# First layer of a four-layer trunk: VectorE's order by a reckoning of two engines' progress

## The chip, the core and the metric

One core of a Trainium2 chip runs the whole program. The metric is device time in microseconds, from the start to the end of one execution; less is better. The engines are TensorE (PE, with its weight loads PEld), VectorE (DVE), ScalarE (ACT), GpSimd (POOL) and SyncE (SP), which issues most transfers.

## What is computed

Four decoder layers with a different token mixer each, over 256 rows of 1024 columns in float32. The change concerns the first layer, native sparse attention: 16 heads of 64 columns, four heads to a key head, three branches (compressed, selected, sliding window), gated and added.

```python
def block(i):                                   # nsa_mixer, 64 query rows at a time
    dist = t[:, None] - cmp_end[None, :]
    p_c = masked_softmax(jnp.einsum('bhgqd,bhnd->bhgqn', qb, kcmp) - slopes * dist.astype(f32), dist >= 0)
    o_c = jnp.einsum('bhgqn,bhnd->bhgqd', p_c, vcmp)
    ...
    p_s = masked_softmax(jnp.einsum('bhgqd,bhqkd->bhgqk', qb, ksel) - slopes * dist.astype(f32), dist >= 0)
    o_s = jnp.einsum('bhgqk,bhqkd->bhgqd', p_s, vsel)
    ...
    p_w = masked_softmax(jnp.einsum('bhgqd,bhkd->bhgqk', qb, kwin) - slopes * dist.astype(f32), mask)
    o_w = jnp.einsum('bhgqk,bhkd->bhgqd', p_w, vwin)
    return jnp.stack([o_c, o_s, o_w])
...
o = jnp.sum(gates * outs, axis=0).reshape(B, S, H * dh)
return (o.astype(u.dtype) * jax.nn.silu(z)) @ w_out
```

`kcmp` and `vcmp` are 15 compressed keys and values for each key head, made by a small two-layer network (`compress`). With 256 rows the selected branch takes every block and the window covers all rows, so both are plain causal attention over their own keys and values.

## The kernel before

**Precision.** A float32 weight is split into a high part (ScalarE, L127, `whi`) and a low part (VectorE, L70, `wlo = raw - whi`, 128x1024), and a product is three matmuls (L234 to L236, or L299 to L301 where the weight is the moving operand). Weights pass through five `raw` buffers: a transfer starts when the low part of the weight five places earlier has been computed. High and low parts have eleven buffers each. `advance` loads weights and issues the high parts, `low_parts` and the first steps of a projection issue the low parts.

**Projections as filler.** `push_proj` puts a projection of 256 output columns into the queue `fq` as 16 steps of three matmuls. `run` goes through a list of work items and calls `fill` after each, which pops some steps (`pop`). So TensorE's order is written out: an item, a step or more, an item.

**The units.** `nsa_order` lists eight units (`nsa_unit`), two heads each; two units make a group g, which shares a key head. A unit's front is `first` (score matmuls L886 and L887 of query rows 0 to 127 for both heads, then VectorE's masks L333), `second` and `finish` (rows 128 to 255, one head each). A mask instruction adds the causal mask, takes the minimum and leaves its result for ScalarE's exponential (L335). Score tiles (`S`) have two buffers: the matmuls of a third tile wait until the masks have read the first. A unit's back runs during the next unit: `trans` (transposes L340, evacuated by ScalarE at L166) twice, then `pvs` (products with v at L356 and L359, the compressed branch's share at L928). The normalisation of a unit's probabilities (`scale`: L905, and L911 eight times) is issued by VectorE after the next unit's first masks.

**The compressed branch.** `cmp_front(g)` stands ahead of a group's first unit: scores of the compressed keys (L829), a reduction (L833), and two lists of five VectorE instructions each in `CHALF`, the halves of its softmax. `first` takes the first half, `second` of the group's first unit the second (L847 to L851). The result `cs` is transposed by `cmp_back(g)` (L864) after `second` of the group's second unit.

**VectorE's order.** In this stretch VectorE's order is the order in which the program issues (`st["own"]`, a manual schedule); ScalarE's is set by the scheduler of the tile framework. `later(n, f)` puts f off until n more steps have been popped; `overdue`, called after each step, issues what is due. Low parts are issued at fixed places: one in `second`, one in `finish`, and ahead of the steps that need them.

**The end of the layer.** `Gate.go` multiplies the output by the gate (L393), `split` makes high and low parts of it (L401, L402), and `out_proj` multiplies by eight output weights (`in_a_o`), 24 matmuls of 512 columns for each half of the columns.

Of the kernel before, what the change touches and what calls it, by code (L numbers as in the profile page):

```python
# [25 lines left out]
NMM, NSB = 3, 2  # L26
KO = (0, 4, 1, 5, 2, 6, 3, 7)
# [9 lines left out]
def trunk(ctx, tc, I, out):  # L37
# [27 lines left out]
    st = {"load": 0, "split": 0, "next": 0, "held": 0, "parts": 0, "after": [], "most": len(seq), "own": False}  # L65
# [11 lines left out]
    def later(n, f):  # L77

        if st["own"]:
            waiting.append((plan["count"] + n, f))  # L80
        else:
            f()

    def overdue(everything=False):
        due = [w for w in waiting if everything or w[0] <= plan["count"]]
        for w in due:
            waiting.remove(w)
            w[1]()
        if due:
            overdue(everything)  # L90

# [157 lines left out]
    def pop():  # L249
        fq.popleft()()  # L250
        plan["count"] += 1
        overdue()
# [6 lines left out]
    def need(i):  # L259

        while fq and (i not in ready or plan["count"] < ready[i] + 6):
            pop()

    def push_proj(use, q=fq, idx=None):

        t = {}
        idx = idx or take(2)

        def step(c, k):
            if c == 0 and k == 0:  # L270
                t["o"] = ps.tile([128, 2, 256], F32, name="mm", bufs=NMM)
            for i, at in ((idx[c], 0), (idx[c] + 1, 0)):
                if k == at and i in low:
                    low.pop(i)()
            wh, wl = parts[idx[c]]
            mm3(t["o"][:, c, :], wh[:, k, :], wl[:, k, :], uT[0][:, k, :], uT[1][:, k, :], k == 0, k == 7)
            if k == 7:
                free(idx[c])
                if c == 1:
                    use(t["o"])  # L280
                advance()

        for c in range(2):
            for k in range(8):
                q.append(lambda c=c, k=k: step(c, k))
# [76 lines left out]
    class Gate:  # L362
# [19 lines left out]
        def have_o(self, p):  # L382
            self.o.add(p)
            self.go()
# [332 lines left out]
    def keep_q(o, g):  # L717


        for j in range(2):  # L720
# [3 lines left out]
            with tc.high_priority(offset=EARLY):  # L724
                ACT.activation(hi, o[r], AF.Copy, scale=sc)
            later(5, lambda r=r, other=other, hs=hs, hi=hi, sc=sc: DVE.scalar_tensor_tensor(
                t["q"][other, hs, :], o[r], sc, hi.bitcast(F32), op0=OP.mult, op1=OP.subtract))
# [5 lines left out]
    def compress(q, lp):  # L733
# [8 lines left out]
        if q == 3 and lp == 3:  # L742
# [6 lines left out]
            def cubic():  # L749
# [3 lines left out]
                later(3, lambda: DVE.scalar_tensor_tensor(hid, ht, 1.0, hp, op0=OP.add, op1=OP.mult))  # L753
# [18 lines left out]
    def second_layer():  # L772
        kp = ps.tile([128, 512], F32, name="S", bufs=NSB)
        for k in range(2):
# [5 lines left out]
                                 op1=OP.subtract)  # L780
        vp = ps.tile([128, 256], F32, name="o", bufs=1)
# [4 lines left out]
        for g in range(4):  # L786
            DVE.tensor_tensor(vbd[g], vp[0:60, None, g * 64:(g + 1) * 64].to_broadcast([60, 4, 64]),
                              bm[:, :, None].to_broadcast([60, 4, 64]), op=OP.mult)
# [33 lines left out]
    def cmp_front(g):  # L822
# [8 lines left out]
        cs = CS[g] = work.tile([128, 2, 4, 15], F32, name="cs", bufs=2)  # L831
        two = sc[:, 0:256].rearrange("p (a s n) -> p a n s", s=2, n=16)[:, :, 0:15, :]
# [28 lines left out]
    def cmp_back(g):  # L861
        ptc = ps.tile([128, 4, 128], F32, name="pt", bufs=2)
# [5 lines left out]
    def nsa_unit(p):  # L868
# [8 lines left out]
        def scores_of(b, js):  # L877
# [4 lines left out]
            for j in js:  # L882
# [5 lines left out]
                S[j] = s  # L888
            for j in js:
                for br in range(2):  # L890
# [4 lines left out]
        def finish():  # L895
            scores_of(1, (1,))
            low_parts(1)
# [16 lines left out]
        def trans(br):  # L914
            t["PT", br] = [transpose_p(t["P"][j, br], "a") for j in range(2)]
# [7 lines left out]
        def pvs():  # L923
            pv(0)
            pv(1)
            o = t["o"]
# [5 lines left out]
        def first():  # L932
            scores_of(0, (0, 1))
            mixed(*(x.pop(0) for x in (SCALE, CHALF) if x))

        def second():
            scores_of(1, (0,))
            if CHALF:
                mixed(CHALF.pop(0))
            low_parts(1)  # L940
# [19 lines left out]

    gh = run(nsa_order(), ga)
    low_parts(len(seq))
# [332 lines left out]
```

## Time and profile before

| | |
|---|---|
| median of 3 runs | 576.66 us (576.42 to 577.11) |
| profiled execution | 576.96 us |
| its span, first to last instruction | 575.3 us |
| PE, PEld busy | 558.5 us, 495.9 us |
| DVE, ACT, POOL busy | 417.3 us, 337.8 us, 32.0 us |
| mean granted clock of TensorE | 0.995 |

The times in the trace count from the start of the span. The first layer's units run from about 69 to 158. A row of the timeline gives start and duration of an instruction, its line, what it writes and reads, and in brackets the idle time ahead of it and what ended that. The ends of matmuls are modelled, so starts are the better measure on PE.

### The profile page before, as it was taken

To read this page: it belongs to the slowest core of one execution; us is meant where nothing else is said; L and a number is where in the kernel's file an instruction comes from. 1 tells how busy PE (TensorE), PEld (TensorE's weight loads), DVE (VectorE), ACT (ScalarE), POOL (GpSimd) and SP (SyncE) were. 2 spreads that over 40 slices of the span, in tenths; PEclk is the share of its full clock that TensorE was granted. 3 is DMA by queue.
4 is the path that set the end of the run, shared out by engine and by line. 5 is a ranking of instruction groups with operands and counts; after the bars stand their busy time and mean duration, and the time that the engine had idled before them with its cause. 6 is when DMAs were issued, how large, how long until landed. Compare 5 with 4: busy or idle time off the path is not lost.

```text
span 575.3 us, 10451 instructions
## 1 busy us (share of the span) xinstructions
PE 558.5 (97%) x3930; PEld 495.9 (86%) x3930; DVE 417.3 (73%) x924; ACT 337.8 (59%) x727; POOL 32.0 (6%) x88
## 2 busy tenths in 40 slices
PE   8999979999999999999999999999999999999995
PEld 7997878777788899999988889999988899899984
DVE  6883796798857877777875896758548878788632
ACT  7752777778925566567633573757525755576410
POOL 2300000000001000001060000000000000000000
PEclk9999989999999999999999999999999999999999
DMA  8764632332443595443432577433525784332012
GB/s 305 252 246 158 246 111 75 122 99 78 152 157 138 187 331 212 148 148 111 159 115 95 184 284 267 158 135 122 171 73 179 271 282 147 121 104 71 2 38 73
DMA packets 27779, 90.96 MB, mean 158 GB/s; under 512 B 4560, under 2 KB 5200, under 8 KB 27728
## 3 DMA queue, kind: packets, MB, share of 16 engines
q1 hardware_dynamic: 26144, 86.09, 43.8%
q10 hardware_dynamic: 1584, 4.20, 2.3%
q8 instruction: 31, 0.51, 0.4%
q14 instruction: 20, 0.16, 0.1%
HBM read 89.22 MB, written 1.05 MB: 157 GB/s over the span
## 4 chain that ended last, share of the span: by engine, by line
PE 86%; DVE 7%; issue 4%; ACT 2%; POOL 1%; POOLq 0%; DVEq 0%; ACTq 0%
PE mm L234 15%; PE mm L235 14%; PE mm L236 14%; PE mm L300 8%; PE mm L301 8%; PE mm L299 8%; PE S L350 3%; PE pt L340 3%; PE o L356 2%; DVE wlo L70 2%; DVE P L333 1%; PE o L737 1%; PE mm L542 1%; PE pt L216 1%; DVE P L911 1%
## 5 line engine op out<-in xcount | busy, mean ns | idle before, releaser
L234 PE MATMUL mm<-uth,whi 128*128 128x256 f32 x736 | 218.2, 296 | 0.0
L70 DVE TENSOR_TENSOR wlo<-raw,whi 128x1024 fp32r<-128x1024 f32 (+1 forms) x153 | 183.1, 1210 | 41.2 <-ACT whi L127 39.8
L235 PE MATMUL mm<-utl,whi 128*128 128x256 f32 x736 | 208.4, 283 | 0.0
L236 PE MATMUL mm<-uth,wlo 128*128 128x256 f32 x736 | 208.3, 283 | 0.0
L127 ACT ACTIVATE whi<-raw 128x1024 fp32r<-128x1024 f32 (+1 forms) x153 | 156.9, 1042 | 65.2 <-PE mm L235 34.2
L234 PEld LDWEIGHTS mm<-uth,whi 128*128 128x128 f32 x736 | 140.8, 191 | 14.1 <-issue 13.3
L235 PEld LDWEIGHTS mm<-utl,whi 128*128 128x128 f32 x736 | 141.3, 192 | 0.9
L236 PEld LDWEIGHTS mm<-uth,wlo 128*128 128x128 f32 x736 | 141.0, 192 | 0.0
L300 PE MATMUL mm<-whi,kT 128*128 128x512 f32 x128 | 50.0, 391 | 1.3 <-DVE kT L402 1.3
L299 PE MATMUL mm<-whi,qT 128*128 128x512 f32 x128 | 50.4, 394 | 0.0
L301 PE MATMUL mm<-wlo,qT 128*128 128x512 f32 x128 | 49.9, 390 | 0.0
L299 PE MATMUL mm<-whi,uth 128*128 128x512 f32 (+1 forms) x112 | 42.6, 380 | 0.0
L301 PE MATMUL mm<-wlo,uth 128*128 128x512 f32 (+1 forms) x112 | 42.1, 376 | 0.0
L300 PE MATMUL mm<-whi,utl 128*128 128x512 f32 (+1 forms) x112 | 42.0, 375 | 0.0
L333 DVE CUSTOM_DVE_ANT_0 P<-S,mask 128x128 f32<-128x128 f32 (+1 forms) x96 | 29.1, 352 | 7.7 <-PE S L887 5.4
L335 ACT ACTIVATE P<-P,mxa 128x128 f32<-128x128 f32 (+1 forms) x64 | 28.4, 446 | 10.1 <-DVE mxa L333 10.0
L468 ACT ACTIVATE junk<-mm 128x512 bf16<-128x512 f32 x16 | 9.5, 594 | 40.2 <-PE mm L301 40.2
L340 PE MATMUL pt<-ident,P 128*128 128x128 f32 x180 | 28.0, 280 | 1.7 <-ACT PT L166 0.8
L300 PEld LDWEIGHTS mm<-whi,kT 128*128 128x128 f32 x128 | 24.1, 188 | 6.3 <-DVE kT L402 1.7
L166 ACT ACTIVATE PT<-pt 128x384 f32<-128x384 f32 x58 | 25.9, 482 | 4.6 <-PE pt L340 4.5
L301 PEld LDWEIGHTS mm<-wlo,qT 128*128 128x128 f32 x128 | 24.0, 188 | 5.0
L299 PEld LDWEIGHTS mm<-whi,qT 128*128 128x128 f32 x128 | 24.1, 188 | 4.7
(212 smaller groups left out, 734.1 us busy)
## 6 DMA issues: line engine op xcount, KB each, us to landing
raw<-in_a_t_dram SPq DMA_DIRECT2D x24, 512.0 KB, 4.6
raw<-in_b_t_dram SPq DMA_DIRECT2D x24, 512.0 KB, 4.7
raw<-in_d_t_dram SPq DMA_DIRECT2D x24, 512.0 KB, 4.4
raw<-in_c_t_dram SPq DMA_DIRECT2D x20, 512.0 KB, 4.7
raw<-in_w_dram SPq DMA_DIRECT2D x8, 512.0 KB, 4.4
raw<-in_a_o_dram SPq DMA_DIRECT2D x8, 512.0 KB, 3.5
raw<-in_b_v_dram SPq DMA_DIRECT2D x8, 512.0 KB, 5.7
raw<-in_b_o_dram SPq DMA_DIRECT2D x8, 512.0 KB, 3.5
```

What stands on the lines that cost most here:

```text
L70: st["lo"] = DVE.tensor_tensor(lo, t, hi.bitcast(F32), op=OP.subtract).ins
L127: ACT.activation(hi, t, AF.Copy)
L166: ACT.activation(dst, src, AF.Copy)
L234: PE.matmul(o, sh, mh, start=first, stop=False)
L235: PE.matmul(o, sh, ml, start=False, stop=False)
L236: PE.matmul(o, sl, mh, start=False, stop=last)
L299: PE.matmul(o, sh, wh[:, j, c0:c1], start=k == 0, stop=False)
L300: PE.matmul(o, sl, wh[:, j, c0:c1], start=False, stop=False)
L301: PE.matmul(o, sh, wl[:, j, c0:c1], start=False, stop=k == 7)
L333: DVE.tensor_tensor_reduce(out=P[:, c0:c1], in0=S, in1=mask[:, c0:c1], scale=-slope, scalar=BIG, op0=OP.add, op1=OP.min, accum_out=mx)
L335: ACT.activation(P[:, c0:c1], P[:, c0:c1], AF.Exp, bias=mx, scale=-1.0, accum_out=l)
L340: PE.transpose(pt[:, i, :], P[:, i * 128:(i + 1) * 128], ident)
```

## The change

A reckoning of the progress of TensorE (`clock["pe"]`) and VectorE (`clock["dve"]`) is kept while the units are issued: `pe()` and `dve()` add durations written into the code. While `st["units"]` is set, `overdue` calls `chores`, which issues a due item, or a low part if none is due, only if VectorE's reckoned time with it stays within 0.5 us (`AHEAD`) of TensorE's. The fixed low parts in `second` and `finish` are gone. The second half of the compressed branch is put off by four steps (`later(4, ...)`, tag `("c", g)`); what is still waiting when `cmp_back(g)` comes is issued there by `flush`. The same holds for q's low halves (tag g, flushed by `need`) and for the four block products of the compressed values (L787, tag "vbd"). A low part is added behind the second layer's k and behind the hidden layer. `have_o` calls `go` two steps later.

```diff
 NMM, NSB = 3, 2
+AHEAD = 0.5
 KO = (0, 4, 1, 5, 2, 6, 3, 7)
...
         add(n + "_o", *range(8))
-    st = {"load": 0, "split": 0, "next": 0, "held": 0, "parts": 0, "after": [], "most": len(seq), "own": False}
+    st = {"load": 0, "split": 0, "next": 0, "held": 0, "parts": 0, "after": [], "most": len(seq), "own": False, "units": False}
     raw, parts, low = {}, {}, {}
...
-    def later(n, f):
+    def later(n, f, tag=None, us=0.6):
         if st["own"]:
-            waiting.append((plan["count"] + n, f))
+            waiting.append((plan["count"] + n, f, tag, us))
         else:
...
     def overdue(everything=False):
+        if st["units"] and not everything:
+            return chores()
         due = [w for w in waiting if everything or w[0] <= plan["count"]]
...
             overdue(everything)
+    def flush(tag):
+        for w in [w for w in waiting if w[2] == tag]:
+            waiting.remove(w)
+            dve(w[3])
+            w[1]()
+    clock = {"pe": 0.0, "dve": 0.0, "S": deque([0.0] * NSB), "exp": 0.0, "P": {}}
+    def pe(us, after=0.0):
+        clock["pe"] = max(clock["pe"], after) + us
+        return clock["pe"]
+    def dve(us, after=0.0):
+        clock["dve"] = max(clock["dve"], after) + us
+        return clock["dve"]
+    def chores():
+        while True:
+            clock["dve"] = max(clock["dve"], clock["pe"] - 1.0)
+            due = [w for w in waiting if w[0] <= plan["count"]]
+            us = due[0][3] if due else 1.15
+            if clock["dve"] + us > clock["pe"] + AHEAD or not (due or low):
+                return
+            dve(us)
+            if due:
+                waiting.remove(due[0])
+                due[0][1]()
+            else:
+                low_parts(1)
...
         plan["count"] += 1
+        pe(0.36)
         overdue()
...
             pop()
+        flush(i)
...
                 if k == at and i in low:
+                    dve(1.15)
                     low.pop(i)()
...
             self.o.add(p)
-            self.go()
+            later(2, self.go)
...
             later(5, lambda r=r, other=other, hs=hs, hi=hi, sc=sc: DVE.scalar_tensor_tensor(
-                t["q"][other, hs, :], o[r], sc, hi.bitcast(F32), op0=OP.mult, op1=OP.subtract))
+                t["q"][other, hs, :], o[r], sc, hi.bitcast(F32), op0=OP.mult, op1=OP.subtract), g, 0.77)
         ready[g] = plan["count"]
...
                 ACT.activation(ht, ht, AF.Tanh, scale=math.sqrt(2.0 / math.pi))
-                later(3, lambda: DVE.scalar_tensor_tensor(hid, ht, 1.0, hp, op0=OP.add, op1=OP.mult))
+                def rest():
+                    DVE.scalar_tensor_tensor(hid, ht, 1.0, hp, op0=OP.add, op1=OP.mult)
+                    low_parts(1)
+                later(3, rest)
...
                                  op1=OP.subtract)
+        low_parts(1)
         vp = ps.tile([128, 256], F32, name="o", bufs=1)
...
         for g in range(4):
-            DVE.tensor_tensor(vbd[g], vp[0:60, None, g * 64:(g + 1) * 64].to_broadcast([60, 4, 64]),
-                              bm[:, :, None].to_broadcast([60, 4, 64]), op=OP.mult)
+            later(0, lambda g=g: DVE.tensor_tensor(
+                vbd[g], vp[0:60, None, g * 64:(g + 1) * 64].to_broadcast([60, 4, 64]),
+                bm[:, :, None].to_broadcast([60, 4, 64]), op=OP.mult), "vbd", 0.34)
...
         cs = CS[g] = work.tile([128, 2, 4, 15], F32, name="cs", bufs=2)
+        pe(1.0, clock["S"].popleft())
+        clock["S"].append(dve(0.35, clock["pe"] + 0.2))
         two = sc[:, 0:256].rearrange("p (a s n) -> p a n s", s=2, n=16)[:, :, 0:15, :]
...
     def cmp_back(g):
+        flush(("c", g))
         ptc = ps.tile([128, 4, 128], F32, name="pt", bufs=2)
...
                 S[j] = s
+                pe(0.24 * (b + 1) + 0.1, clock["S"].popleft())
             for j in js:
+                clock["S"].append(dve((0.42, 0.69)[b], clock["pe"] + 0.2))
+                clock["exp"] = max(clock["exp"], clock["dve"]) + (0.8, 1.0)[b]
                 for br in range(2):
...
             scores_of(1, (1,))
-            low_parts(1)
             SCALE.append(scale())
...
         def trans(br):
+            pe(0.7, clock["P"].get(p, 0.0))
             t["PT", br] = [transpose_p(t["P"][j, br], "a") for j in range(2)]
...
         def pvs():
+            if p == 0:
+                flush("vbd")
             pv(0)
             pv(1)
+            pe(2.1)
             o = t["o"]
...
         def first():
+            exp = clock["exp"]
             scores_of(0, (0, 1))
+            if SCALE:
+                clock["P"][p - 1] = dve(2.0, exp)
+            if CHALF:
+                dve(1.3)
             mixed(*(x.pop(0) for x in (SCALE, CHALF) if x))
...
             if CHALF:
-                mixed(CHALF.pop(0))
-            low_parts(1)
+                half = CHALF.pop(0)
+                later(4, lambda: mixed(half), ("c", g), 1.1)
...
+    st["units"] = True
+    clock["pe"] = clock["dve"] = 0.0
     gh = run(nsa_order(), ga)
+    st["units"] = False
     low_parts(len(seq))
```

The order of instructions shows what comes of it. TensorE's order is the same in both kernels, instruction by instruction. VectorE's changes, and ScalarE's (by its scheduler) with it. Line numbers after the change are higher: the masks are L372, the low parts L71, the scaling L956 and L962, the second half L895 to L899, the compressed transposes L913, the block products L832, the tanh gate L481 and L432, the gate's low part L441.

VectorE in group 0, from the second masks of unit 0 (`S_1009`) to the first of unit 1 (`S_1073`), before. `cl` and `cs` are the second half, `wlo` are low parts, `qT` q's low halves, `S_1047` the third scores of unit 0:

```order
L333 ISA P_978,mxa_982<-S_1009,mask_306 128x256
...
L847 TENSOR_REDUCE cl_961<-cs_958 128x8
...
L851 TENSOR_TENSOR cs_958<-cs_958,cl_961 128x120
L70 TENSOR_TENSOR wlo_762<-raw_759,whi_761 128x1024
L726 SCALAR_TENSOR_TENSOR qT_841<-mm_869,cq_304,qT_841 64x2x256 x2
L333 ISA P_979,mxa_982<-S_1047,mask_306 128x256
...
L70 TENSOR_TENSOR wlo_767<-raw_764,whi_766 128x1024
L333 ISA P_1067,mxa_1072<-S_1073,mask_315 128x128
```

The same place after (the tiles are now `S_1006`, `S_1038` and `S_1065`; `v_364` are block products):

```order
L372 ISA P_975,mxa_979<-S_1006,mask_306 128x256
...
L832 TENSOR_TENSOR v_364<-o_937,bm_355 60x256
L71 TENSOR_TENSOR wlo_762<-raw_759,whi_761 128x1024
L372 ISA P_976,mxa_979<-S_1038,mask_306 128x256
...
L832 TENSOR_TENSOR v_364<-o_937,bm_355 60x256 x2
L372 ISA P_1059,mxa_1064<-S_1065,mask_315 128x128
```

The second half and q's low halves are gone from between the second and the third masks.

VectorE in the second unit of group 1 (unit 3), before: the last scaling of unit 2, the second masks of unit 3 (`S_1410`), a low part, the third masks (`S_1479`); the second half of this group stands 27 rows earlier, in unit 2:

```order
L911 TENSOR_SCALAR P_1232<-P_1232,la_1233 128x256
L333 ISA P_1374,mxa_1379<-S_1410,mask_315 128x256
...
L333 ISA P_1375,mxa_1379<-S_1410,mask_315 128x256
...
L70 TENSOR_TENSOR wlo_863<-raw_802,whi_862 128x1024
L333 ISA P_1376,mxa_1379<-S_1479,mask_315 128x256
```

After, at the same place:

```order
L962 TENSOR_SCALAR P_1231<-P_1231,la_1232 128x256
L372 ISA P_1366,mxa_1371<-S_1402,mask_315 128x256
...
L895 TENSOR_REDUCE cl_1220<-cs_1217 128x8
...
L899 TENSOR_TENSOR cs_1217<-cs_1217,cl_1220 128x120
L71 TENSOR_TENSOR wlo_800<-raw_784,whi_799 128x1024
L372 ISA P_1368,mxa_1371<-S_1476,mask_315 128x256
```

TensorE there, after (and, but for names and lines, before): the second scores of unit 3, two steps, and the transposes of `cs_1217`, which L899 above writes.

```order
L935 MATMUL S_1402<-kT_470,qT_841 128x512
L936 MATMUL S_1402<-tu_471,qT_841 128x512
L270 MATMUL mm_1287<-uth_88,whi_776 128x256
L271 MATMUL mm_1287<-utl_89,whi_776 128x256
L272 MATMUL mm_1287<-uth_88,wlo_777 128x256
L270 MATMUL mm_1287<-uth_88,whi_776 128x256
L271 MATMUL mm_1287<-utl_89,whi_776 128x256
L272 MATMUL mm_1287<-uth_88,wlo_777 128x256
L913 MATMUL pt_1420<-ident_77,cs_1217 60x128 x2
```

The second half now stands behind the scaling and the second masks, in groups 0, 2 and 3 too (in group 0 with one low part more ahead of it).

VectorE at the end of the units, before: gate (`zw`, L442 and L393) and its low parts (`kT`) for the last quarter, then low parts of weights, the first of them of the seventh output weight (`raw_1187`):

```order
L402 TENSOR_TENSOR kT_2012<-oT_868,qT_2011 128x512 x3
...
L442 SCALAR_TENSOR_TENSOR zw_2111<-zw_2111,mm_1981 128x512
L393 SCALAR_TENSOR_TENSOR oT_868<-oT_868,zw_2111 128x512
L402 TENSOR_TENSOR kT_2012<-oT_868,qT_2011 128x512
L70 TENSOR_TENSOR wlo_1709<-raw_1187,whi_1708 128x1024
```

After (`raw_839` is the first output weight, `raw_1031` the fifth):

```order
L441 TENSOR_TENSOR kT_2006<-oT_869,qT_2005 128x512
L71 TENSOR_TENSOR wlo_1108<-raw_839,whi_1107 128x1024
L71 TENSOR_TENSOR wlo_1180<-raw_865,whi_1179 128x1024
L71 TENSOR_TENSOR wlo_1283<-raw_900,whi_1282 128x1024
L481 SCALAR_TENSOR_TENSOR zw_2108<-zw_2108,mm_1975 128x512
L432 SCALAR_TENSOR_TENSOR oT_869<-oT_869,zw_2108 128x512
L441 TENSOR_TENSOR kT_2006<-oT_869,qT_2005 128x512
L71 TENSOR_TENSOR wlo_1357<-raw_967,whi_1356 128x1024
L71 TENSOR_TENSOR wlo_1449<-raw_1031,whi_1448 128x1024
```

The low parts of the first six output weights have moved from inside the units to behind their last scaling.

## Rows read from the trace of the kernel before

**Rows 1.** The page: busy time and share; clock over the span's 40 slices; exponentials.
```profile
PE 558.5 (97%) x3930; PEld 495.9 (86%) x3930; DVE 417.3 (73%) x924; ACT 337.8 (59%) x727; POOL 32.0 (6%) x88
...
PEclk9999989999999999999999999999999999999999
...
L335 ACT ACTIVATE P<-P,mxa 128x128 f32<-128x128 f32 (+1 forms) x64 | 28.4, 446 | 10.1 <-DVE mxa L333 10.0
```

**Rows 2.** PE's waits, 60 to 165: who for whom, us in total, times, longest.
```profile
PE S L886 <- DVE mxa L333: 4.3, 5, 2.1
PE pt L340 <- ACT PT L166: 0.8, 2, 0.4
```

**Rows 3.** Timeline of PE in group 0: start us, duration us, instruction.
```profile
77.18 0.28 PE L887 MATMUL S<-tu,qT 128*128 128x256 f32 x1
79.56 0.36 PE L886 MATMUL S<-kT,qT 128*128 128x256 f32 x1 [2.11 <-DVE mxa L333]
...
83.00 0.63 PE L864 MATMUL pt<-ident,cs 128*60 128x128 f32 x2
...
86.22 0.82 PE L340 MATMUL pt<-ident,P 128*128 128x128 f32 x6
```

**Rows 4.** Timeline of DVE in group 0.
```profile
69.04 1.41 DVE L787 TENSOR_TENSOR v<-o,bm 60x256 f32<-60x256 f32 x4 [0.63 <-PE o L784]
...
74.69 0.27 DVE L847 TENSOR_REDUCE cl<-cs 128x8 f32<-128x120 f32 x1
...
75.64 0.28 DVE L851 TENSOR_TENSOR cs<-cs,cl 128x120 f32<-128x120 f32 x1
```

**Rows 5.** Stretch 81 to 85: busy us of each engine, granted clock, DMA share, GB/s.
```profile
81.00:85.00 4.00, 3.88 (x18) 3.70 (x19) 3.93 (x19) 3.23 (x11) 0.00 (x0) 0.57 0.38 135
```

**Rows 6.** Timeline of DVE in unit 3.
```profile
104.64 0.28 DVE L333 CUSTOM_DVE_ANT_0 P<-S,mask 128x128 f32<-128x128 f32 x1
...
105.48 0.20 DVE L905 RECIPROCAL la<-la 128x8 f32<-128x8 f32 x1
...
107.77 0.41 DVE L333 CUSTOM_DVE_ANT_0 P<-S,mask 128x256 f32<-128x256 f32 x1
...
108.45 1.22 DVE L70 TENSOR_TENSOR wlo<-raw,whi 128x1024 fp32r<-128x1024 f32 x1
```

**Rows 7.** Timeline of PE in units 3, 5 and 7.
```profile
105.28 0.47 PE L886 MATMUL S<-kT,qT 128*128 128x512 f32 x1 [0.80 <-DVE mxa L333]
...
106.54 0.38 PE L864 MATMUL pt<-ident,cs 128*60 128x128 f32 x2
...
110.60 0.40 PE L886 MATMUL S<-kT,qT 128*128 128x512 f32 x1
...
125.44 0.47 PE L886 MATMUL S<-kT,qT 128*128 128x512 f32 x1 [0.63 <-DVE mxa L333]
...
144.75 0.47 PE L886 MATMUL S<-kT,qT 128*128 128x512 f32 x1
...
145.64 0.38 PE L864 MATMUL pt<-ident,cs 128*60 128x128 f32 x2
...
148.93 0.40 PE L886 MATMUL S<-kT,qT 128*128 128x512 f32 x1
...
153.40 0.82 PE L340 MATMUL pt<-ident,P 128*128 128x128 f32 x6
```

**Rows 8.** Instructions on the raw weights, 55 to 165: ns least, median, most.
```profile
L127 ACT ACTIVATE whi<-raw x25: 1040/1049/1071, 57.0 to 160.8; 128x1024 fp32r<-128x1024 f32 x25
...
DMA to landing us min/median/max: 3.4/3.5/5.3
```

**Rows 9.** Timelines of PE and DVE in the output projection.
```profile
165.30 0.39 PE L301 MATMUL mm<-wlo,qT 128*128 128x512 f32 x1
...
165.18 5.76 DVE L70 TENSOR_TENSOR wlo<-raw,whi 128x1024 fp32r<-128x1024 f32 x5
```

## Prediction

> **Names.** In the first layer eight units of two heads run in four groups, 0 to 3; a group's two units share a key head. A unit's scores come in three parts: F1 (query rows 0 to 127, both heads), F2 and F3 (rows 128 to 255, one head each, 512 columns). T0 and T1 are the two transposes of a unit's probabilities, run during the next unit. Each group has one compressed branch, whose softmax is two halves on VectorE (five instructions each). Its result, `cs`, is transposed by L864 after F2 of the group's second unit. A step is one entry of the projection queue: three matmuls.
>
> **What bounds the kernel now.** I read the page's engine shares first: TensorE is busy for 97% of the span and VectorE for 73% [rows 1]. So only TensorE's waits, and the time its clock is halved, can be won, and a delay counts when TensorE stands behind it. Next come TensorE's waits in the first layer [rows 2]: five before scores, 4.3 us, all ended by VectorE, and two before transposes, 0.8 us. The longest lies in group 0. TensorE has issued the first pair of score matmuls of unit 1 at 77.18 and gets the next score buffer only at 79.56 [rows 3]. On VectorE at that time stand the second half (74.69 to 75.92), a weight's low part and two q low parts [rows 4], and only behind them the F3 masks that free the buffer. After this wait the granted clock falls: its mean over 81 to 85 is 0.57 [rows 5], so about 3.4 of these 4 us ran at the lower level of 1.2 GHz, half of the upper one, and 1.7 us of work was lost.
>
> **Part 1: the second half moves behind the next unit's scaling.** The order of the changed kernel shows it at the same place in all four groups: not in a gap of VectorE, but by the flush ahead of the compressed transposes. It stands behind the second unit's F1 masks, the scaling of eight blocks and the F2 masks. TensorE's order is unchanged, so L864 must wait for that chain. I cost it in group 1, where every link has a row. Let s be the start of the F1 masks of unit 3, 104.64. The reciprocal and the scaling start at 105.48, the F2 masks at 107.77, and the instruction behind them at 108.45, s+3.81 [rows 6]. The half lasts 1.23 us (74.69 to 75.92, [rows 4]), so L864 can start at s+5.04. TensorE starts F2 at 105.28, s+0.64, and L864 1.26 us later, s+1.90 [rows 7]. New wait: 3.14 us. In groups 2 and 3 there is one step instead of two between F2 and L864 (144.75 to 145.64 is 0.89 us, [rows 7]), and the wait is 3.51 us each. Sum for groups 1 to 3: 10.2 us. It can't be hidden by VectorE running ahead, because s itself waits for TensorE's F1.
>
> Some of it is given back. While TensorE stands, ScalarE and VectorE catch up. The 0.63 us wait before F2 in group 2 [rows 7] goes, since no low parts stand ahead of its F1 masks any more; group 1 keeps its 0.80, because the gate product L393 now stands ahead of F1 and waits for the output of unit 1. From L864 to F3 takes 4.06 us in group 1 (106.54 to 110.60) and 3.29 in group 3 (145.64 to 148.93) [rows 7]; with T1's waits on evacuations and scaling gone I take 3.7 and 2.6, and 2.6 in group 2 as well, which returns 0.4 + 0.7 + 0.7. Net for groups 1 to 3: 10.2 - 0.6 - 1.8 = 7.8 us; bounds 6 and 10.2 (nothing returned).
>
> **Part 2: group 0.** Here the change does what its reckoning aims at. Between the F2 and F3 masks of unit 0 stand only one block product (1.41 us for four, [rows 4]) and one low part, so the three waits of this group go, 2.9 us (the 4.3 of [rows 2] less the 0.80 and 0.63 of groups 1 and 2, [rows 7]), and TensorE reaches L864 by 79.3: 83.00 [rows 3] less 2.9 and 0.8 for the part of the cold stretch that lies ahead of it. VectorE's queue to the end of the half, counted from the end of the F2 masks of unit 0 (74.69 before, about 0.8 earlier now, since three of the four block products moved behind): three block products 1.05, two low parts 2.3 (five take 5.76, [rows 9]), F3 masks 0.68 (as F2's, [rows 6]), F1 masks 0.84, reciprocal and scaling 2.29, F2 masks 0.68, the half 1.23, together 9.07. That is 82.9 to 83.8. L864 starts where it started before, 83.0, and the gain ahead of it is spent. Behind it, T1 can't beat 86.4: the second low part now ends at about 81.9 and releases the transfer of a raw weight; that lands 3.5 us later, its high part takes 1.05 us on ScalarE [rows 8], and in ScalarE's new order it stands ahead of the evacuation that T1 needs. T1 was at 86.22 [rows 3], so group 0 costs +0.2 at least, and +1.4 if the clock falls once more. I take +0.7.
>
> **Part 3: low parts left over.** Before, six of the eight output weights have their low part ahead of the units' last scaling; now the first stands behind it. Two things follow. In unit 7 the F3 exponentials stand behind a high part on ScalarE whose transfer is released by the low part after the half of group 3: L864 + 1.15 + 3.5 + 1.05, then two exponentials of 0.45 [rows 1] and half of the 2.29 for reciprocal and scaling make T0 at L864 + 7.8. Before, it was 7.76 (145.64 to 153.40, [rows 7]), and 7.1 with the 0.7 returned in part 1. That is +0.7. In the output projection the fifth output weight is read at 165.30; the run of low parts behind the last gate split starts at 165.18 [rows 9], and its low part is now the second of that run: 165.18 + 2 x 1.15 = 167.5. That is 2.2 us of waiting, or 1.4 if the gate chain, freed of the high part ahead of it on ScalarE, comes 0.8 earlier. I take 1.9. Sum +2.6; bounds 0.5 (both covered by other slack) and 4.
>
> **Part 4: the clock.** The one wait above 2 us was followed by 3.4 us at half clock, and none of the other waits, 0.8 us or less, was [rows 2]: the clock row of the page has its only lower digit there [rows 1]. The three new waits of 3.1 to 3.5 us are longer than the one that cost 1.7. I charge two of three, 3.5 us; bounds 0 and 5.2. The Trainium skill (TensorE: Matmul & The Clock Gate, section "HAM oscillation — how this bites in real kernels") describes a loop in which every wait for data is followed by a cold start and takes half of each throttled stretch as the penalty. By it all four waits of this kernel would be charged, group 0 too, and the sum would be some 2.4 us higher; the one case in this trace agrees with its price, and whether every wait falls cold no row here shows.
>
> **The sum.** 7.8 + 0.7 + 2.6 + 3.5 = 14.6 us on the profiled execution of 576.96, that is 591.6. That execution lies 0.3 above the median of 576.66, so I predict 591.3.
>
> **Rivals.** (a) The clock holds in groups 1 to 3 and the tail is covered: 7.8 + 0.2 + 0.5 = 8.5 us, 585. For it: a wait's fall in clock is seen once only. Against: the new waits are longer than that one.
>
> (b) Faster: L864's wait vanishes, because VectorE stands so far ahead that the half is done when TensorE arrives, and the waits before scores go with the cold stretch: 4.3 + 0.8 + 1.7 = 6.8 us at most, 570. The point from which it decides: the half would have to end by s+1.90, yet the scaling and F2 masks ahead of it alone end at s+3.81. VectorE's idle stretches do exist, but they lie behind L864, and the half isn't put there. 5%.
>
> (c) The change doesn't do what it says and no time moves: the half is put by a flush, not by the reckoning, and each new wait is paid by an old one as in group 0; 577. Groups 1 to 3 have only 1.4 us of such waits before scores, so this holds for group 0 alone. 4%.
>
> **How the numbers follow.** Forecast 66%, (a) 25%, (b) 5%, (c) 4%. The forecast's own range: 6 + 0.2 + 0.5 + 1.7 = 8.4 at the low end, 10.2 + 1.4 + 4 + 5.2 = 20.8 at the high end, hardly all at once. The range reaches down through (a) and stops at 582; up to 598. A measurement of this kernel can tell about 0.2% from no change. Faster 5%, same 4%, slower 91%.
>
> **What would show it.** Right: L864 waits some 3 us for VectorE's L851 in groups 1 to 3 and about 4 in group 0; the 2.1 us wait at 77 is gone; VectorE's idle time before F3 masks grows; the clock shows stretches of 0.5 behind the waits; the first low-part wait in the output projection is on the fifth weight. Wrong: if L864 starts less than 1.5 us behind its step, the chain of part 1 is mis-sized. If the clock stays at 1.00 in groups 1 to 3, part 4 falls and (a) is the time. If the output projection has no wait for a low part, part 3 is halved.

## The result, and the profile after

The changed kernel takes 596.46 us (594.41 to 598.10 in four runs), the kernel before 576.54 beside it: a ratio of 1.0342, with a 95% interval of 1.0326 to 1.0358. The profiled execution took 597.39 us, 20.43 more than that of the kernel before (576.96).

The page of the changed kernel, busy time and granted clock, against [rows 1]:

```profile
PE 565.5 (95%) x3930; PEld 502.1 (84%) x3930; DVE 417.4 (70%) x924; ACT 340.2 (57%) x727; POOL 32.0 (5%) x88
...
PEclk9999979898899899999999999999999999999999
```

VectorE does the same work (417.3 before) and has more idle time; TensorE's share falls. Where the clock row had one low digit, it now has five, all in the first layer and at its end (a slice is 14.9 us).

TensorE's waits from 60 to 200, who for whom, us in total, times, longest, against [rows 2]:

```profile
PE pt L913 <- DVE cs L899: 14.2, 4, 4.2
PE pt L252 <- DVE tu L243: 2.0, 1, 2.0
PE mm L340 <- DVE wlo L71: 1.4, 1, 1.4
PE S L935 <- DVE mxa L372: 1.1, 2, 0.8
```

L913 are the compressed transposes (L864 before), L899 is the last instruction of the half (L851 before). Their four waits are the first row; they did not wait at all before. The 2.1 us wait of [rows 3] before the scores of unit 1 is gone, as are two more of [rows 2].

VectorE in unit 3, start and duration, against [rows 6]:

```profile
106.62 0.28 DVE L372 CUSTOM_DVE_ANT_0 P<-S,mask 128x128 f32<-128x128 f32 x1
...
107.26 0.20 DVE L956 RECIPROCAL la<-la 128x8 f32<-128x8 f32 x1
...
109.54 0.41 DVE L372 CUSTOM_DVE_ANT_0 P<-S,mask 128x256 f32<-128x256 f32 x1
...
110.23 0.27 DVE L895 TENSOR_REDUCE cl<-cs 128x8 f32<-128x120 f32 x1
...
111.18 0.28 DVE L899 TENSOR_TENSOR cs<-cs,cl 128x120 f32<-128x120 f32 x1
111.38 1.22 DVE L71 TENSOR_TENSOR wlo<-raw,whi 128x1024 fp32r<-128x1024 f32 x1
117.51 0.42 DVE L372 CUSTOM_DVE_ANT_0 P<-S,mask 128x256 f32<-128x256 f32 x1 [4.91 <-PE S L936]
```

The chain is the one the prediction reckoned: F1 masks, scaling, F2 masks, the half at 110.23. Its result is there at 111.46; TensorE had reached the transposes at 108.49. The last row shows what that buys: VectorE then stands idle for 4.91 us, waiting for the F3 scores that TensorE could not reach. VectorE's lateness is made by its order, not by its load.

What followed each wait, by the granted clock (1.00 is 2.4 GHz, 0.50 is 1.2 GHz; columns as in [rows 5]):

```profile
112.00:116.00 4.00, 4.00 (x23) 4.00 (x23) 0.60 (x1) 2.01 (x6) 0.00 (x0) 0.58 0.42 131
136.00:140.00 4.00, 4.00 (x23) 3.96 (x23) 0.95 (x1) 2.25 (x5) 0.00 (x0) 0.59 0.38 130
160.00:164.00 4.00, 4.00 (x23) 3.99 (x22) 0.64 (x1) 2.58 (x6) 0.00 (x0) 0.61 0.43 161
```

Each mean stands for more than three of the four us at the lower level, and in group 0 the clock was at 0.50 from 83.2 to 88. And there is a place the prediction doesn't speak of, the border between the first layer and the second. Timelines of ScalarE, VectorE and TensorE there:

```profile
187.28 2.17 ACT L163 ACTIVATE whi<-raw 128x1024 fp32r<-128x1024 f32 x2 [5.12 <-DMA raw<-in_b_v_dram]
189.35 0.58 ACT L507 ACTIVATE junk<-mm 128x512 bf16<-128x512 f32 x1
...
188.38 2.36 DVE L71 TENSOR_TENSOR wlo<-raw,whi 128x1024 fp32r<-128x1024 f32 x2 [3.29 <-ACT whi L163]
190.65 0.15 DVE L509 TENSOR_SCALAR poh<-ss 128x1 f32<-128x1 f32 x1
...
197.18 1.07 PE L252 MATMUL pt<-ident,tu 128*128 128x128 f32 x4 [2.01 <-DVE tu L243]
```

The squares of the output (L507) and the chain of the norm (L509) stand in ScalarE's and VectorE's order behind the high and low parts of the second layer's first weights (`in_b_v`), which wait for their transfers. TensorE waits 2.01 us for the result, and the clock falls once more (0.66 over 198 to 202).

### The profile page after: what moved, and what is told of

Read it like the earlier page. It is cut to its first block, busy times and chain, and to the rows that moved or that the text cites. A ratio compares the mean times of both kernels' runs of the same rounds, so it can differ in the third digit from the quotient of the medians.

```text
span 595.7 us, 10434 instructions
## 1 busy us (share of the span) xinstructions
PE 565.5 (95%) x3930; PEld 502.1 (84%) x3930; DVE 417.4 (70%) x924; ACT 340.2 (57%) x727; POOL 32.0 (5%) x88
## 4 chain that ended last, share of the span: by engine, by line
PE 80%; DVE 9%; issue 4%; DMA 3%; ACT 2%; POOL 1%; POOLq 0%; DVEq 0%; SPq 0%; ACTq 0%
PE mm L270 15%; PE mm L271 13%; PE mm L272 13%; PE mm L339 7%; PE mm L340 7%; PE mm L338 7%; PE pt L379 4%; PE S L389 3%; PE o L395 2%; DVE P L372 2%; DVE P L962 2%; DVE wlo L71 1%; PE o L776 1%; DMA raw<-in_b_v_dram 1%; PE pt L252 1%
## 5 line engine op out<-in xcount | busy, mean ns | idle before, releaser
L71 DVE TENSOR_TENSOR wlo<-raw,whi 128x1024 fp32r<-128x1024 f32 (+1 forms) x153 | 182.7, 1210 | 43.8 <-ACT whi L163 42.8
L372 DVE CUSTOM_DVE_ANT_0 P<-S,mask 128x128 f32<-128x128 f32 (+1 forms) x96 | 29.1, 352 | 25.1 <-PE S L936 22.9
L379 PE MATMUL pt<-ident,P 128*128 128x128 f32 x180 | 31.1, 303 | 0.7
L507 ACT ACTIVATE junk<-mm 128x512 bf16<-128x512 f32 x16 | 9.5, 592 | 31.2 <-PE mm L340 31.2
```

The source lines that it names most:

```text
L71: st["lo"] = DVE.tensor_tensor(lo, t, hi.bitcast(F32), op=OP.subtract).ins
L372: DVE.tensor_tensor_reduce(out=P[:, c0:c1], in0=S, in1=mask[:, c0:c1], scale=-slope, scalar=BIG, op0=OP.add, op1=OP.min, accum_out=mx)
L379: PE.transpose(pt[:, i, :], P[:, i * 128:(i + 1) * 128], ident)
```

## The experiments

**Theory A**: the time is TensorE's wait for the half, which stands behind the second unit's scaling and F2 masks, and the half clock behind each wait. **Theory B**: the later low parts of the weights hold up transfers and high parts, and the waits at L913 only show it. Ratios are to the kernel before on the same chip (medians 577.03, 577.33 and 577.23 us), with 95% intervals.

| Kernel | us | ratio |
|---|---|---|
| e1, half at once | 576.89 | 1.0001 [0.9990, 1.0013] |
| e2, half late, alone | 599.82 | 1.0392 [1.0375, 1.0410] |
| e3, low parts back | 599.25 | 1.0390 [1.0345, 1.0436] |
| e4, both back | 575.28 | 0.9975 [0.9965, 0.9985] |
| e5, wait filled | 592.62 | 1.0263 [1.0247, 1.0278] |
| e6, transposes behind T1 | 582.08 | 1.0087 [1.0070, 1.0104] |
| e7, half at once, 1.0 us ahead | 573.25 | 0.9933 [0.9919, 0.9948] |
| e8, half ahead of the scaling | 574.99 | 0.9963 [0.9950, 0.9975] |
| e9, only 1.0 us ahead | 579.92 | 1.0045 [1.0031, 1.0060] |
| e10, e8 and 1.0 us ahead | 573.78 | 0.9943 [0.9930, 0.9955] |

### One part undone, one part alone (e1, e2)

```diff
 # e1, in second(), against the changed kernel
-                half = CHALF.pop(0)
-                later(4, lambda: mixed(half), ("c", g), 1.1)
+                dve(1.1)
+                mixed(CHALF.pop(0))
 # e2, against the kernel before: in second(), then ahead of and in cmp_back()
-                mixed(CHALF.pop(0))
+                t_half[g] = CHALF.pop(0)
...
+    t_half = {}
+
     def cmp_back(g):
+        mixed(t_half.pop(g))
```

> The changed kernel with one part undone: the second half of a compressed softmax is issued right behind the F2 masks of the group's first unit, as in the kernel before; block products, query low parts and weight low parts stay under the reckoning. Theory A (the half behind the next unit's scaling and F2 masks makes TensorE wait, and the clock falls behind each such wait): the four waits of the compressed transposes, 14.2 us in the changed kernel, go, and with them the stretches at half clock in groups 1 to 3, 13.3 us in all by the shift of the scores of the trace; group 0 even gains up to 3 us, since its waits before scores stay away; the loss behind the layer (output projection 1.6, layer border 4) remains. Time 576 to 581 us. Theory B (the weights' low parts, later in VectorE's queue, hold up the transfers and high parts, and the waits of the compressed transposes only show it): the time stays at 590 us or more.

> The kernel before with one part of the change alone: the second half is issued ahead of the compressed transposes, behind the second unit's scaling and F2 masks. Low parts and everything else keep their fixed places, so a low part of a weight still stands behind the F2 masks and now ahead of the half. Theory A: the compressed transposes wait 3 to 4.5 us in all four groups, a stretch at half clock follows each wait, and the time is 588 to 596 us, with no wait in the output projection and none of 2 us at the layer border. Theory B: 577 to 581 us, because the low parts come in time.

e1 has no wait at L913 and, in the profiled execution, no low digit in its clock row. TensorE's waits from 60 to 200:

```profile
PE S L935 <- DVE mxa L372: 3.0, 3, 2.2
PE pt L252 <- DVE tu L243: 1.1, 1, 1.1
...
PE mm L340 <- DVE wlo L71: 0.2, 1, 0.2
```

One instruction group moved back takes away the whole loss of 20 us. The loss behind the units, which I expected to stay at 5.6 us, shrank to 2.5: from the F3 scores of unit 7 to the transposes at the border (L252) it takes 32.04 us, against 29.53 in the kernel before, with a wait of 0.2 us and one of 1.1 without half clock. So more than half of that loss was a consequence of the late half too. Why is not shown; a late half may take the room in which the reckoning would have handed out low parts, but only one more of them stands ahead of the last gate split (14 against 13). The scores of group 3 come 3 us earlier than before, and most of that is lost again by the border. e2 is the reverse, the half late and nothing else:

```profile
PE pt L867 <- DVE cs L851: 17.5, 4, 4.5
PE S L889 <- DVE mxa L333: 2.1, 4, 1.0
```

It loses 22.8 us, more than the whole change and more than the 588 to 596 expected, with no wait in the output projection and none at the border. The reason for the larger waits is in VectorE's order, here in unit 5:

```profile
138.43 1.22 DVE L70 TENSOR_TENSOR wlo<-raw,whi 128x1024 fp32r<-128x1024 f32 x1
139.57 0.27 DVE L847 TENSOR_REDUCE cl<-cs 128x8 f32<-128x120 f32 x1
```

A low part at its fixed place stands ahead of the half, 1.14 us here (waits of 4.53 and 4.54 in groups 2 and 3 against 3.40 and 3.39; 4.16 in group 1 against 3.12). So theory B falls twice: the half alone makes the loss, and the half alone takes it away.

### The low parts at their places (e3, e4)

```diff
 # chores(): no low parts; both kernels
-            if clock["dve"] + us > clock["pe"] + AHEAD or not (due or low):
+            if clock["dve"] + us > clock["pe"] + AHEAD or not due:
                 return
...
 # finish(), and the same two lines at the end of second()
+            dve(1.15 if low else 0.0)
+            low_parts(1)
 # rest() in compress(), second_layer()
-        low_parts(1)
 # e4: and second() as in e1
```

> The changed kernel with the weights' low parts at the fixed places of the kernel before (one behind the F2 masks and one behind the F3 masks of every unit), the half still late. Theory A: the wait for the fifth output weight and the wait at the layer border with its stretch at half clock go, 5.3 to 5.6 us; the waits of the compressed transposes stay or grow by 1.15 us where a low part now stands ahead of the half. Time 590 to 594 us. Theory B: 580 us or less.

> The changed kernel with both undone: half at once and low parts at their fixed places; block products and query low parts are still put off until they are needed. Theory A: no losses are left, and the gain of the change is seen alone: the 2.9 us of waits before scores in group 0 and the 1.7 us of its cold stretch go at least in part. Time 572 to 576 us, against 576.5 before. Theory B gives no time below that of the kernel before.

e3 missed: 599.25 us, with times from 596.35 to 602.17. What was expected to go did go: its trace (of the execution of 596.35) has no wait for a low part in the output projection and none at the border. But other waits came:

```profile
PE pt L908 <- DVE cs L894: 13.4, 3, 4.5
PE o L392 <- DVE v L827: 2.3, 1, 2.3
PE S L870 <- DVE qT L762: 1.4, 2, 0.9
```

With low parts at fixed places the halves of groups 0, 2 and 3 have one ahead of them, and a block product (L827) and query low parts (L762) come too late; in group 1 the half is issued ahead of the second unit's F1 masks, and nothing waits for it. What separates e3's four times no trace shows; the mean granted clock is 0.977 in the first two and 0.971 and 0.972 in the others (601.10 and 602.17). e4 gives 575.28 us, inside 572 to 576: a quarter of a per cent below the kernel before. That is what the rest of the change is worth without the late half. The gain lies in group 0: from the F2 scores of unit 0 to the F3 scores of unit 1 it takes 12.41 us (74.45 to 86.86), against 15.13 before (72.46 to 87.59), and no clock falls there (the clock row of its page is all nines). The profiled execution, at 576.91 us the longest of ten, had come 2 us late to the units.

### The clock by itself (e5)

```diff
 # cmp_back(), against the changed kernel
         ptc = ps.tile([128, 4, 128], F32, name="pt", bufs=2)
+        for _ in range((36, 26, 28, 28)[g]):
+            PE.transpose(ptc[:, 2, :], ident, ident)
```

> The changed kernel with TensorE kept busy while its compressed transposes wait: ahead of them it runs 36, 26, 28 and 28 transposes of the identity (groups 0 to 3, about 0.1 us each at full clock) into a part of the same PSUM tile that nobody reads. Extra work that is not needed; the half still comes late. It takes the clock alone out of the loss. Theory A with the clock as a price of its own: the stretches behind the four waits run at full clock, which gives back some 1.6 us in each of groups 1 to 3 and 1.5 to 2 in group 0. Time 588 to 592 us. If the granted clock costs nothing, because VectorE and ScalarE set the pace behind the wait: 595 to 598 us.

TensorE in unit 3, and the stretches behind the waits of groups 1 to 3:

```profile
106.23 3.00 PE L913 MATMUL pt<-ident 128*128 128x128 f32 x26
109.53 0.38 PE L915 MATMUL pt<-ident,cs 128*60 128x128 f32 x2 [0.30 <-ACT P L374]
```

```profile
110.00:114.00 4.00, 4.00 (x35) 3.90 (x33) 0.65 (x2) 2.67 (x6) 0.00 (x0) 1.00 0.39 137
132.00:136.00 4.00, 3.77 (x29) 3.30 (x29) 1.56 (x3) 2.93 (x7) 0.00 (x0) 1.00 0.37 119
155.00:159.00 4.00, 4.00 (x34) 3.38 (x35) 0.66 (x1) 3.41 (x8) 0.00 (x0) 1.00 0.37 91
```

The clock stays at 1.00, so the clock's share can be read off group by group. Start of the F3 scores of each group's second unit:

| unit | before | after | e5 | after minus e5 |
|---|---|---|---|---|
| 1 | 87.59 | 89.12 | 87.03 | 2.09 |
| 3 | 110.60 | 116.84 | 113.21 | 3.63 |
| 5 | 129.62 | 140.07 | 135.08 | 4.99 |
| 7 | 148.93 | 163.79 | 157.43 | 6.36 |

The clock takes 2.1, 1.5, 1.4 and 1.4 us in the four groups, 6.4 together. What is left of the shift in e5, 8.50 us by unit 7, is the waits alone. The time of the profiled executions fell by 4.59 us (597.39 to 592.80; the medians, each less that of the kernel before on its own chip, by 4.63), less than 6.4. Most of the rest is given back to later waits. At the border ScalarE's wait for the transfer of `in_b_v` grew from 5.12 to 6.42 us and TensorE's from 2.01 us to this row's, and in the output projection TensorE's grew from 1.40 to 1.58:

```profile
PE pt L252 <- DVE tu L243: 3.1, 1, 3.1
```

### Where the half, or its reader, has to stand (e6, e8)

```diff
 # e6, nsa_order()
             if p % 2:
-                order.append(lambda p=p: cmp_back(p // 2))
-            order += [*b[:2], f[2], b[2]]
+                order.append(lambda p=p: flush(("c", p // 2)))
+            order += b[:2]
+            if p % 2:
+                order.append(lambda p=p: cmp_back(p // 2))
+            order += [f[2], b[2]]
 # e8, first()
             scores_of(0, (0, 1))
+            if p % 2:
+                flush(("c", g))
             if SCALE:
```

> The changed kernel with TensorE's order altered at one place: the half is still put off and flushed ahead of the second unit's T0, as before, but the compressed transposes stand behind T1 instead of ahead of T0, so that T0 and T1, whose blocks are scaled ahead of the half, run while VectorE does the half. Theory A (the wait costs because the compressed transposes stand ahead of work that could run): the waits of the compressed transposes shrink below 1 us, no stretch at half clock is left in groups 1 to 3, and the time is 576 to 583 us. Rival: T0 waits for the scaling as long as the compressed transposes did, since VectorE is what is late; 588 us or more.

> The changed kernel with the half still put off to the group's second unit but flushed behind its F1 masks, ahead of the scaling of the eight blocks: 3 us earlier in VectorE's queue than in the changed kernel, a whole unit later than in the kernel before. By theory A it ends 2.1 us behind the start of the F1 masks, and TensorE reaches the compressed transposes 1.9 us behind it: waits of 0 to 1 us, no half clock, and at most 1.2 us a group because the scaling, and T0 with it, now stands behind the half; 577 to 583 us. If being put off by a unit is what costs, wherever it stands: 588 us or more.

e6 leaves the half as late as it was in groups 0 to 2, by the flush, and gives TensorE T0 and T1 to do meanwhile; in group 3 the reckoning, whose course is altered by this, places the half itself behind the masks of the group's first unit. Its waits, 60 to 200:

```profile
PE S L935 <- DVE mxa L372: 2.8, 2, 2.4
PE mm L340 <- DVE wlo L71: 1.3, 1, 1.3
PE pt L252 <- DVE tu L243: 1.2, 1, 1.2
PE pt L913 <- ACT P L374: 0.9, 1, 0.9
PE pt L913 <- DVE cs L899: 0.7, 1, 0.7
```

No wait at L913 is above 0.9 us and the time is 582.08, inside 576 to 583: most of what the late half cost came from its reader standing ahead of work that could run. Not all of it went: e6 is 0.87% above the kernel before. Its F3 scores of unit 7 start at 148.85 (148.93 before, but 143.61 in e8), and the transposes at the border at 182.10 (178.46), so against the kernel before the loss lies behind the units. In e8 the half of groups 0 and 2 is flushed 3 us further ahead in VectorE's queue, still in the second unit; those of groups 1 and 3 the reckoning now places behind the F3 masks of the first unit. It has 574.99 us, two us below what was expected and 0.4% below the kernel before. Its only wait of this kind:

```profile
PE pt L913 <- DVE cs L899: 0.4, 1, 0.4
```

So in the two groups where the half still stands in the second unit, being put off costs nothing that shows; what cost was that it stood behind the scaling and the F2 masks.

### One number (e7, e9, e10)

```diff
 # e9, against the changed kernel; e10 is e9 with the edit of e8, e7 with that of e1
-AHEAD = 0.5
+AHEAD = 1
```

> The half at once, as in e1, and the reckoning lets VectorE run 1.0 us ahead of TensorE instead of 0.5, which hands out 18 low parts ahead of the last gate split where e1 hands out 14 and the kernel before 16. In e1 the scores of group 3 came 3 us earlier than in the kernel before and the layer border gave 2 of them back to two low parts that stood ahead of the norm's chain. If the late low parts are what takes the gain back: no wait at the layer border, 573 to 575.5 us. If not, or if the low parts ahead delay the masks: 576 us or more.

> The changed kernel with one number altered: the reckoning lets VectorE run 1.0 us ahead of TensorE instead of 0.5. In its order the halves of groups 1 to 3 are then put by the reckoning, between the masks of the group's first unit, and no longer by the flush; only that of group 0 still comes behind the second unit's scaling. Low parts ahead of the last gate split: 18, against 13 in the changed kernel and 16 in the kernel before. Theory A (the loss hangs on where the half lands, and the tail on the low parts left over): one wait of the compressed transposes is left, that of group 0, 4.3 us with its half clock; none in groups 1 to 3; no wait above 1 us at the layer border; 575 to 579 us. If putting the half off costs by itself: 585 us or more.

> As e9 (1.0 us ahead), and a half that the reckoning has not placed by then is flushed behind the F1 masks of the second unit, ahead of the scaling, as in e8; that concerns group 0 alone. Theory A: no compressed transposes wait over 1 us, no half clock in the layer, no wait at the border; 572.5 to 574.5 us, level with e7 (573.25). Otherwise, if a half put off keeps a price: 575 us or more.

In the code, an item of 1.1 us is handed out when VectorE's reckoned time plus 1.1 is at most TensorE's plus `AHEAD`. With 0.5 VectorE must be reckoned 0.6 us behind TensorE when the half is first among the due items, and in the changed kernel that happens in no group before the flush; with 1.0 it takes 0.1. In e9 the half of group 1 goes between the F2 and the F3 masks of unit 2, where VectorE was idle, and those of groups 2 and 3 behind the F3 masks of units 4 and 6. VectorE in unit 2:

```profile
101.05 0.09 DVE L372 DVE_READ_ACCUMULATOR2_ANT mxa<- 128x1 f32 x1
101.80 0.28 DVE L895 TENSOR_REDUCE cl<-cs 128x8 f32<-128x120 f32 x1 [0.66 <-ACT cs L893]
...
103.01 0.42 DVE L372 CUSTOM_DVE_ANT_0 P<-S,mask 128x256 f32<-128x256 f32 x1
```

One wait is left of four, that of group 0, whose half still comes by the flush, with its half clock; and none is left in the output projection or at the border (16 low parts stand ahead of the last gate split, as in the kernel before; I had expected 18):

```profile
PE pt L913 <- DVE cs L899: 4.3, 1, 4.3
PE pt L379 <- ACT PT L202: 0.6, 2, 0.4
```

579.92 us is just above the 575 to 579 expected. e10 takes that last wait too and has 573.78 us: the difference, 6.1 us, is the price of a single late half in group 0 (4.26 us of wait and a clock of 0.56 over the 6 us behind it; the F3 scores of unit 1 start at 90.08 and 84.01), with nothing ahead of it that swallows a part. e7 reaches 573.25 us by the other way, with the half at once. The two longest rows of e10's waits from 60 to 200 and its clock row:

```profile
PE S L935 <- DVE mxa L372: 0.7, 2, 0.6
PE S L819 <- DVE P L808: 0.4, 1, 0.4
...
PEclk9999999999999999999999999999999999999998
```

e7 and e10 beat both kernels, by 0.67% and 0.57% against the kernel before. In e1 (`AHEAD` 0.5) 14 low parts stood ahead of the last gate split and the time was that of before; in e7 18 do, and the wait at the border is gone. From the F3 scores of unit 7 to the border's transposes it takes 32.04 us in e1, 29.74 in e7 and 29.53 before. That the late low parts took back e1's gain is borne out by this pair.

## Why the prediction was right, and where it was not

Predicted 591.3 us, measured 596.46, inside the range of 582 to 598 and slower, by the mechanism named. By its terms, on the profiled executions (20.4 us apart; the medians are 19.9 apart):

| Term | predicted | measured |
|---|---|---|
| Part 1, groups 1 to 3, without the clock | 7.8 | 9.1 |
| Part 2, group 0, without the clock | 0.7 | -0.6 |
| Part 3, T0 of unit 7 | 0.7 | 0 |
| Part 3, fifth output weight | 1.9 | 1.6 |
| Part 4, clock in the groups | 3.5 | 6.4 |
| Layer border | none | 4.0 |
| Sum | 14.6 | 20.4 |

**Part 1** held link by link: waits of 3.12, 3.40 and 3.39 us against 3.14, 3.51 and 3.51. What TensorE gets back behind them is seen in e5, without the clock: L915 to F3 takes 3.68, 2.85 and 2.85 us, against 3.7, 2.6 and 2.6. The net is taken from the table of e5 (8.50 at unit 7, less -0.56 at unit 1) and is 1.3 above the forecast: groups 2 and 3 got back 0.44 us each and not 0.7, the 0.63 us wait before F2 in group 2 was said to go and stayed at 0.35, and some 0.5 us lie in small steps that I did not separate.

**Part 2**: the wait of L913 was 4.25 us ("about 4"), and it started at 83.22 against 83.0. The three waits ahead went, and L913 was where it had been. Behind it the forecast was 0.7, between 0.2 with the clock holding and 1.4 with a fall. Measured are 1.53 with the fall and -0.56 without it (e5): the bound by which T1, behind a raw weight's transfer, could not come earlier was too high (86.4; it starts at 85.66 in e5), and the clock's part too low. Parts 1 and 2 together, 8.5 us both forecast and measured, agree by luck: two errors cancel.

**Part 3**: the wait on the fifth output weight came as forecast, 1.40 us and a shift of 1.57. The 0.7 for T0 of unit 7 did not come: T0 kept its distance to the F3 scores (the shift is 14.86 at both; in e5 8.50 and 8.74), though a high part does stand ahead of the F3 exponentials on ScalarE. The step that failed here is its end: the low parts left over were counted to the last output weight and not beyond. The same lateness reaches the next layer's first weights, whose high and low parts the orders place ahead of the norm's chain at the border. L252 starts 2.3 us later than by the shift before it (197.18 and 178.46 against 16.43), and the half clock behind that wait takes another 1.7: 4.0 us in all (0.66 over the 4 us from 198 makes 1.4 of it). That it hangs on the low parts being late is borne out by e3 and e9, in which they come early enough and the border has no wait, and by e5, where TensorE comes earlier and waits longer.

**Part 4** was mis-sized in number, not in price. The price of 1.7 us read from the one cold stretch of the kernel before stands between the 1.4 and 2.1 measured. I charged two waits; all four were followed by the lower level, and the one at the border too. The loop that the Trainium skill describes, which the prediction set beside its own count (TensorE: Matmul & The Clock Gate, section "HAM oscillation — how this bites in real kernels"), is one in which each wait for data is followed by a cold start. For these four waits it was the better forecast: with the 2.4 us more that the prediction named for it, 3.5 becomes 5.9, and the trace has 6.4. Shorter waits did not follow it every time (see the end). Rival (a), in which the clock holds, falls with part 4.

Rivals (b) and (c) did not come about, for the reason given: in the changed kernel the flush placed every half. With one number changed (e9) the reckoning places the halves of groups 1 to 3, and their waits go, as (b) has it: VectorE's idle stretches, which the prediction saw only behind L864, also lie between and behind the masks of the group's first unit. A time below the kernel before takes group 0 as well (e10).

In all, the forecast of 14.6 us fell short of the 20.4 by the clock (2.9) and the border (4.0), and came inside its range by the range's width, which had been reckoned without the border.

## What to carry to other kernels

An order made by a reckoning is as good as its slack: look in the order at whether an item was placed by the reckoning or by its deadline, and let the deadline stand ahead of the long work that follows, not behind it. When an engine of secondary load is made to finish something late, look for what the bound engine has queued behind the reader; moving the reader behind other ready work took away most of the loss here (e6), moving the writer all of it (e1, e8). Follow lateness past the end of the stage: what is left over there stands in front of the next stage's short chain.

## What the runs showed of the hardware

A wait's length did not tell whether the clock falls. In the kernel before, a wait of 2.11 us [rows 3] was followed by half clock [rows 5], and in the changed kernel the 2.01 us at the border was. In e1 a wait of 2.22 us before scores at 102.81, and in e6 one of 2.45 us at 103.48, were not. The stretch behind the first, in e1, and that behind the second, in e6:

```profile
103.00:105.00 2.00, 2.00 (x17) 1.91 (x17) 1.93 (x11) 1.74 (x9) 0.00 (x0) 1.00 0.74 248
```

```profile
104.00:106.00 2.00, 2.00 (x17) 1.79 (x16) 1.96 (x10) 1.10 (x5) 0.00 (x0) 1.00 0.00 0
```

In e3 one of 2.29 us at 93.62 was not either, and behind two shorter ones, 0.88 and 0.51 us at 145.36 and 146.15, the clock fell:

```profile
147.00:150.00 3.00, 3.00 (x13) 2.90 (x14) 1.96 (x14) 1.59 (x8) 0.00 (x0) 0.50 0.03 5
```

The waits of 3.1 us and more were all followed by it. Each trace is one execution, and whether a wait is followed by half clock may differ between executions of one kernel: of e1's ten, the profiled one and four others have a mean clock of 0.998 or 0.999 and take 575.95 to 576.25 us, the other five 0.995 or 0.996 and 577.52 to 577.84. By an estimate from these figures, 0.003 of 576 us is 1.7 us, about the price of one such stretch; that the five had one is not shown, as no trace of them was kept.

Transposes whose result nobody reads kept the clock at 1.00 in the groups (e5), but of the 6.4 us that this saved 1.8 were lost again by the end.
